# E table of an S5 layer on VectorE alone, and its output tables made during the latents' S5 projections

## The chip, the cores and the metric

The kernel runs on one core of one Trainium2 chip. The metric is the device time of one execution in microseconds (us); smaller is better. A core has a matrix engine (TensorE, "PE" in the rows, "PEld" for its weight loads), three elementwise engines (VectorE "DVE", ScalarE "ACT", GpSimd "POOL") and a queue engine (SyncE "SP") that issues the transfers (DMAs). Each engine works through its own instructions strictly in order and waits on the others through semaphores.

## The reference, cut to what matters

One layer of a diffusion backbone over 1024 latent tokens and 256 context tokens of width 1024: a half-step SwiGLU FFN, a mixer (a gated short convolution beside a bidirectional S5 state-space scan with 32 groups of 64 complex states), and a second FFN.

```python
x = half_step_ffn(x, mods[0:3], ...); ctx = half_step_ffn(ctx, mods_c[0:3], ...)
lam_bar = jnp.exp(lam * dt)
b_bar = ((lam_bar - 1.0) / lam)[:, :, None] * b
c_mat = lax.complex(c_re, c_im)
...
bu = jnp.einsum('blgh,gph->blgp', ug, b_bar)
_, h = lax.associative_scan(_linear_recurrence, (a, bu), axis=1, reverse=reverse)
y = einsum('blgp,ghp->blgh', states, c_mat).real + ... + d_skip * ug
...
x = half_step_ffn(x, mods[6:9], ...)
```

## The kernel before, in words

**Tiling.** Tokens are taken in chunks of 8, so the scan runs over 128 latent chunks (and 32 context chunks) instead of 1024 tokens. What a chunk does to the state and to the output is put into tables made from the S5 parameters: B (8 powers of lam_bar times b_bar), C (8 powers times c), E (32 x 4 powers that turn the scan into one over real magnitudes), F and T. B, C, E and F lie in one DRAM tensor, `pd`, in column ranges BO, CO, EO and FO, one block for each of 16 pairs of groups; T lies in `td`.

**Order of the work.** (1) `g_lat`, the latents' gate/up product of the first FFN. Each of 22 column blocks is seven products of 12 matmuls, since every fp32 operand is split into a high and a low half: ScalarE copies the high half (`w<-t`, `w<-wr` on ACT), VectorE subtracts it for the low half (the same names on DVE). Raw weights come by DMA into four buffers `wr`. (2) `g_ctx`, the same for the 256 context rows, with 24 matmuls of 256 columns for each 128 columns of weights. (3) The down products. (4) In `run`, `u_lat`: the latents' S5 inputs, two groups of four 24-matmul products, stored to `ud` and read back into `tb`; beside them `ctx_in` sums, norms, scales and transposes the context rows, and `u_ctx` projects them. (5) Convolution products with the 16 S5 pairs (`s5_pair`) between them; each pair loads its block of `pd`. (6) Output projection and second FFN.

**Where the tables are made.** `s5_params` is a generator that makes E and F and stores the powers (`pwd`) and b_bar (`brd`). `fill` in `run` advances it from inside `g_lat`: each `self.step(fills[m - 1])` asks for as many steps as FN holds for the product, 12 for a column block, and between two yields of `s5_params` stand SP[n] empty steps, before 1 and 2 in turn. For E eight iterations each make two halves of 128x512, `er` and `ei` (real and imaginary), with a temporary `xt`: six products or sums, on VectorE in even iterations and on GpSimd in odd ones, then two stores to `pd`. `er`, `ei` and `xt` are the same memory in every iteration. In the rows all of this is `tb<-tb 128x512` and `pd<-tb`. `s5_prep` makes B, T and then C, advanced from inside `g_ctx`. C is four iterations of six instructions of 128x1024 (`z<-z,z`), on VectorE and GpSimd in turn, with two stores each (`pd<-z`). T goes over DRAM: small stores `gd<-z`, then `td<-gd`.

**What sets the order.** The kernel is written as above, but a scheduler with a simulated timeline orders each engine's instructions from the dependences and priorities; `step` gives fill work lower priority. All DMAs here go through SP's one queue in order, so a DMA that waits holds up those behind it. All instructions are recorded through one helper, so every row says L51: rows are told apart by tiles (w split halves, wr raw weights, ps PSUM, t and z scratch, tb the five-row buffer).

Of the kernel before, what the change touches and what calls it, by code (L numbers as in the profile page):

```python
# [16 lines left out]
P = 128  # L17
D = 1024
# [8 lines left out]
H = 16  # L27
T8 = 8
# [40 lines left out]
class Kernel:  # L69
# [111 lines left out]
    def setup(self):  # L181
        nc, i = self.nc, self.i
        self.cp = self.pool("cp")
        self.dr = self.pool("dr", space=bass.MemoryType.DRAM)
        self.psum = self.pool("psum", bufs=8, space=bass.MemoryType.PSUM)
        self.sm = self.pool("sm", bufs=8)
        self.wp = self.pool("wp", bufs=6)
        self.tp = self.pool("tp", bufs=1)
        self.tb = self.t(self.tp, [P, 5 * D], "tb")
        self.ring([self.tb[:, D * k : D * k + D] for k in range(5)])  # L190
        self.wrs = [self.t(self.wp, [P, D], f"wr{k}", bufs=1) for k in range(4)]
        self.zp = self.pool("zp", bufs=32)

        dr = self.dr
        self.x1d = self.t(dr, [T8, CL, D], "x1d")
        self.x2d = self.t(dr, [T8, CL, D], "x2d")
        self.rowd = [self.t(dr, [KT, P], f"rowd{k}") for k in range(4)]
        self.pd = self.t(dr, [PAIRS, P, TO], "pd")
        self.pwd = self.t(dr, [P, D], "pwd")
        self.brd = self.t(dr, [P, D], "brd")  # L200
        self.gd = self.t(dr, [H, G, 15, H], "gd")
        self.td = self.t(dr, [P, G, P], "td")
        self.ud = self.t(dr, [G * H, T8, CL], "ud")
        self.ucd = self.t(dr, [G * H, T8, CC], "ucd")
        self.yd = self.t(dr, [T8, H, G, CL], "yd")
        self.zd = [self.t(dr, [P, NT], f"zd{k}") for k in range(4)]
        self.t1d = [self.t(dr, [P, 512], f"t1d{k}") for k in range(NF // 2)]
        self.t2d = [self.t(dr, [P, 512], f"t2d{k}") for k in range(NF // 2)]
        self.scd = [self.t(dr, [P, 4 * NC], f"scd{k}") for k in range(6)]
        self.sd = [[self.t(dr, [P, NT], f"sd{n}_{k}") for k in range(NF)] for n in range(2)]  # L210

        cp = self.cp
        rows = self.t2([16, P])
        self.load(rows[0:8, :], i["c"][0].rearrange("(k p) -> k p", p=P))
        self.load(rows[8:16, :], i["c_ctx"].rearrange("(k p) -> k p", p=P))
        self.ident = self.t(cp, [P, P], "ident")
        make_identity(self.tc.nc, self.ident)
        srow = self.t2([16, P])
        nc.scalar.activation(srow, rows, AF.Silu)
        pt = self.ps()  # L220
        self.tr(pt[:, :16], srow, 16)
        self.scol = self.t(cp, [P, 16], "scol")
        nc.vector.tensor_copy(self.scol, pt[:, :16])
        self.srep = self.t(cp, [P, KT, 32], "srep")
        nc.scalar.activation(
            self.srep.rearrange("p k (n c) -> p n c k", c=2),
            pt[:, :16].rearrange("p (c k) -> p c k", c=2).unsqueeze(1).to_broadcast([P, 16, 2, KT]), AF.Copy,
        )
        self.ones = self.t(cp, [P, 1], "ones")
        nc.gpsimd.memset(self.ones, 1.0)  # L230
        self.modc = {}
        self.mask = self.t(cp, [P, 2 * CL + 4], "mask", dt=mybir.dt.bfloat16)
        nc.gpsimd.memset(self.mask, 1.0)
        nc.gpsimd.memset(self.mask[:, :: CL + 1], 0.0)
# [939 lines left out]
    def s5_params(self):  # L1174
        nc, i = self.nc, self.i
        pl = nc.gpsimd
# [4 lines left out]
        def A(n):  # L1181
            v = arena[:, used[0] : used[0] + n]
            used[0] += n
            assert used[0] <= D
            return v
# [28 lines left out]
        e, em1, s, cm1 = A(64), A(64), A(64), A(64)  # L1214
# [8 lines left out]
        pw = pv[:, :576].rearrange("p (r m a) -> p r m a", r=2, m=9)  # L1223
# [88 lines left out]
        pdv = self.pd.rearrange("a p w -> p a w")  # L1312
        for r in range(2):
            for b in range(2):
                gs = slice(16 * b, 16 * b + 16)
# [19 lines left out]
        for b in range(8):  # L1335
            gs = slice(4 * b, 4 * b + 4)
            er, ei, xt = (
                u.rearrange("p (a m n) -> p a m n", a=4, m=4) for u in (ee[:, :512], ee[:, 512:], arena[:, :512])
            )
            shp = [P, 4, 4, 32]  # L1340
            x0 = e32[0][:, gs, :].unsqueeze(2).to_broadcast(shp)
            x1 = e32[1][:, gs, :].unsqueeze(2).to_broadcast(shp)
            v0 = vv[:, 0, :, gs].rearrange("p m a -> p a m").unsqueeze(3).to_broadcast(shp)
            v1 = vv[:, 1, :, gs].rearrange("p m a -> p a m").unsqueeze(3).to_broadcast(shp)
            self.cmul(er, ei, x0, x1, v0, v1, xt, pl if b % 2 else None)
            for r, m in ((0, er), (1, ei)):
                c0 = EO + 256 * r
                self.load(
                    pdv[:, 2 * b : 2 * b + 2, c0 : c0 + 256], m.rearrange("p (a q) m n -> p a (q m n)", q=2)
                )  # L1350
            yield
# [11 lines left out]
        shp = [P, T8, 32]  # L1363
# [18 lines left out]
    def s5_prep(self):  # L1382
        nc, i = self.nc, self.i
        pl = nc.gpsimd
        slot = lambda shape: self.t(self.zp, shape, "z")
# [4 lines left out]
        pw, br_ = slot([P, 2, 2, T8, 32]), slot([P, 2, 32, H])  # L1390
# [4 lines left out]
        ct = slot([P, 2, 32, H])  # L1395
# [4 lines left out]
        for k in range(2):  # L1400
# [4 lines left out]
            for d in range(2):  # L1405
                r = slice(64 * d, 64 * d + 64)
# [3 lines left out]
        pdv = self.pd.rearrange("a p w -> p a w")  # L1410
        shp = [P, 8, T8, H]

        def power(w, r, gs):
            return pw[:, w, r, :, gs].rearrange("p t a -> p a t").unsqueeze(3).to_broadcast(shp)

        for o in range(4):
            gs = slice(8 * o, 8 * o + 8)
            xr, xi, xt = slot(shp), slot(shp), slot(shp)
# [38 lines left out]
        for t in range(T8):  # L1457
            r = slice(t * H, t * H + H)
# [6 lines left out]
        for t in range(T8):  # L1465
            r = slice(t * H, t * H + H)
            self.load(self.td[r], self.gd[:, :, 7 - t : 15 - t].rearrange("h g l k -> h g (l k)"))
            if t % TY == TY - 1:
                yield
        for o in range(4):  # L1470
            gs = slice(8 * o, 8 * o + 8)
            mr, mi, xt = slot(shp), slot(shp), slot(shp)
            prb, pib = power(1, 0, gs), power(1, 1, gs)
            cr_ = ct[:, 0, gs, :].unsqueeze(2).to_broadcast(shp)
            ci_ = ct[:, 1, gs, :].unsqueeze(2).to_broadcast(shp)
            e = pl if o % 2 else None
            self.mul(mr, cr_, prb, e)
            self.mul(xt, ci_, pib, e)
            self.add(mr, mr, xt, e)
            yield  # L1480
            self.mul(mi, ci_, prb, e)
            self.mul(xt, cr_, pib, e)
            self.sub(mi, mi, xt, e)
            for r, m in ((0, mr), (1, mi)):
                c0 = CO + 256 * r
                self.load(
                    pdv[:, 4 * o : 4 * o + 4, c0 : c0 + 256], m.rearrange("p (a q) t h -> p a (q t h)", q=2)
                )
            yield
# [225 lines left out]
    def run(self):  # L1715
# [13 lines left out]
        xt = [self.z() for _ in range(4)]  # L1729
# [39 lines left out]
        h = self.hops(stages, bl, hb, hr)  # L1769
# [4 lines left out]
        def norm2():  # L1774
            ss = self.t(self.sm, [P, 4], "ss")
            for k in range(4):
                self.square(ss, k, xt2[k])
                yield
            r = yield from self.rsq_g(ss)
            yield  # L1780
            for k in range(4):
                self.scale(xt2[k : k + 1], r[:, k : k + 1], nc.scalar if k in X2A else None)
                yield

        def accs2():
            pt = self.ps()
            for kt in range(KT):
                for mod in range(2):
                    self.first_mm(pt, mod, kt, self.ws[kt][:, mod, :])
            yield  # L1790
            self.first_cols(1, pt)
            yield

        q, a = norm2(), accs2()
# [20 lines left out]
        def fill():  # L1815
# [10 lines left out]
            for n, _ in enumerate(self.s5_params()):  # L1826
                for _ in range(1 + SP[n % len(SP)]):
                    yield
# [86 lines left out]
        u = self.tb.rearrange("p (g c) -> p g c", g=G)  # L1915
        cx = ctx_in()
        next(cx)
        for _ in itertools.chain(self.u_lat(mhi, mlo, 0, u), self.u_lat(mhi, mlo, 1, u)):
            next(cx, None)
        for _ in cx:  # L1920
            pass
        self.u_ctx(chi2, clo2)
# [6 lines left out]
        z = [None] * 4  # L1929
# [103 lines left out]
        p = evac(0, self.out_group(ss[0], wo2))  # L2033
# [4 lines left out]
        p = evac(1, self.out_group(ss[1], wo2))  # L2038
# [7 lines left out]
        p = evac(2, acc)  # L2046
# [5 lines left out]
        h = self.hops(stages, bl, hb, hr)  # L2052
        next(h)
        next(p)
        p = evac(3, acc)
# [64 lines left out]
FW = 22  # L2120
FN = (2, 2, 1, 1, 2, 2, 2)
GAP = 6
SP = (1, 2)
UN2 = 3
EARLY2 = 4
TAIL = 3
# [47 lines left out]
```

## Time and profile before

| | |
|---|---|
| median of three runs | 2077.2 us (2076.4 to 2079.46) |
| the profiled execution | 2077.89 us |
| its span, first to last instruction | 2076.1 us |
| TensorE busy | 1961.8 us, 94% |
| VectorE busy | 1433.3 us, 69% |
| ScalarE busy | 825.3 us, 40% |
| GpSimd busy | 191.3 us, 9% |
| mean granted TensorE clock | 0.98 of 2.4 GHz |

The rows further down come from this one execution. "[2.25 <-ACT t L51]" at a row's end means: the engine stood idle for 2.25 us before this row and was released by ScalarE's instruction that wrote a tile t. A row with "xN" is N neighbouring instructions of one form merged; its time runs from the first start to the last end, and neighbours on one engine overlap a little.

### The profile page before, as it was taken

How to read it: one execution, taken by the hardware profiler on the slowest of the kernel's cores; microseconds unless marked ns; L12 is line 12 of the kernel's file. 1: busy time of each engine (PE TensorE's matmuls, PEld its weight loads, DVE VectorE, ACT ScalarE, POOL GpSimd, SP SyncE). 2: the span in 40 equal slices, each digit the busy share in tenths (PEclk: the TensorE clock that was granted, in tenths of full speed). 3: DMA queues.
4: the chain of work that ended last, by engine and by line, in shares of the span. 5: the costliest groups of instructions: out<-in, count | busy, mean ns of one | idle time of the engine just before them, and what ended most of it. 6: DMA issues, size and time to landing. Idle time of an engine off the chain costs nothing. (4 is left out here: it accounts for less than half of the span.)

```text
span 2076.1 us, 25812 instructions
## 1 busy us (share of the span) xinstructions
PE 1961.8 (94%) x9364; PEld 1562.7 (75%) x9364; DVE 1433.3 (69%) x2532; ACT 825.3 (40%) x1459; POOL 191.3 (9%) x106
## 2 busy tenths in 40 slices
PE   7899999989898999999998899997999999999997
PEld 3477778867898877777887778763788888887775
DVE  1874469787766679787528985486865555577977
ACT  5433333423343345566532334353333333334543
POOL 0000000040347000000003430010000000000000
PEclk9999999999999999999999999999999999999999
DMA  9167632445579977476665533134632322267554
GB/s 325 31 218 249 240 137 72 132 127 167 172 222 268 294 249 251 147 259 224 180 207 170 182 112 122 53 130 122 203 122 81 100 73 82 87 254 267 198 182 162
DMA packets 334059, 356.78 MB, mean 172 GB/s; under 512 B 47024, under 2 KB 248428, under 8 KB 333932
## 3 DMA queue, kind: packets, MB, share of 16 engines
q1 hardware_dynamic: 331628, 346.75, 51.4%
q10 hardware_dynamic: 2304, 8.39, 1.0%
q8 instruction: 73, 1.20, 0.2%
q14 instruction: 54, 0.44, 0.1%
HBM read 282.97 MB, written 74.17 MB: 172 GB/s over the span
## 5 line engine op out<-in xcount | busy, mean ns | idle before, releaser
L51 PE MATMUL ps<-z,w 128*128 128x512 f32 (+1 forms) x5328 | 1151.2, 377 | 39.6 <-DVE w L51 13.1
L51 PEld LDWEIGHTS ps<-z,w 128*128 128x128 f32 x5328 | 937.7, 192 | 236.4 <-DVE w L51 14.9
L51 PE MATMUL ps<-w,w 128*128 128x512 f32 x1848 | 427.3, 392 | 16.3 <-DVE w L51 9.7
L51 PEld LDWEIGHTS ps<-w,w 128*128 128x128 f32 x1848 | 346.4, 188 | 95.6 <-DVE w L51 14.7
L51 ACT ACTIVATE w<-wr 128x512 fp32r<-128x512 f32 (+1 forms) x270 | 206.6, 767 | 348.4 <-PE ps L51 281.7
L51 DVE TENSOR_TENSOR w<-wr,w 128x512 fp32r<-128x512 f32 (+1 forms) x264 | 246.9, 937 | 117.4 <-ACT w L51 110.8
L51 ACT ACTIVATE w<-t 128x512 fp32r<-128x512 f32 x292 | 177.1, 626 | 213.4 <-DVE t L51 129.9
L51 DVE TENSOR_TENSOR w<-t,w 128x512 fp32r<-128x512 f32 x292 | 198.6, 691 | 77.0 <-ACT w L51 76.6
L51 DVE TENSOR_TENSOR t<-t,ps 128x512 f32<-128x512 f32 x150 | 102.4, 684 | 97.6 <-PE ps L51 94.5
L51 PE MATMUL ps<-z,t 128*128 128x512 f32 x512 | 148.0, 449 | 11.4 <-DVE t L51 10.3
L51 ACT ACTIVATE t<-ps 128x512 f32<-128x512 f32 (+2 forms) x143 | 77.4, 542 | 166.3 <-PE ps L51 162.8
L51 PEld LDWEIGHTS ps<-z,t 128*128 128x128 f32 x512 | 96.8, 190 | 60.8 <-issue 36.2
L51 ACT ACTIVATE w<-z 128x512 fp32r<-128x512 f32 x110 | 69.6, 632 | 146.2 <-PE ps L51 144.0
L51 DVE TENSOR_TENSOR z<-z,z 128x512 fp32r<-128x512 f32 (+3 forms) x127 | 106.6, 869 | 15.5 <-ACT z L51 11.6
L51 DVE TENSOR_TENSOR t<-wr 128x512 f32<-128x512 f32 x140 | 94.2, 686 | 32.2 <-DMA wr<-in_ffn_w_gu 18.1
L51 ACT ACTIVATE t<-z 128x1024 bf16<-128x1024 f32 (+3 forms) x132 | 75.5, 605 | 47.2 <-DVE z L51 30.8
L51 DVE TENSOR_TENSOR w<-z,w 128x512 fp32r<-128x512 f32 x110 | 75.5, 686 | 26.6 <-ACT w L51 26.4
L51 POOL TENSOR_TENSOR z<-z,z 128x1024 f32<-128x1024 f32 x24 | 79.2, 3320 | 76.3 <-PE ps L51 42.0
L51 ACT ACTIVATE t<-t 128x512 f32<-128x512 f32 (+1 forms) x83 | 51.7, 623 | 78.6 <-DVE t L51 78.2
L51 DVE TENSOR_TENSOR z<-t,ps 128x512 f32<-128x512 f32 (+1 forms) x52 | 29.8, 573 | 64.9 <-PE ps L51 64.3
L51 POOL TENSOR_TENSOR tb<-tb 128x512 f32<-128x512 f32 x24 | 33.6, 1412 | 435.4 <-DMA sd<-z 409.0
L51 ACT ACTIVATE z<-z 128x512 fp32r<-128x512 f32 (+2 forms) x76 | 48.3, 673 | 56.7 <-DVE z L51 56.7
(121 smaller groups left out, 1402.1 us busy)
## 6 DMA issues: line engine op xcount, KB each, us to landing
wr<-in_ffn_w_gu SPq DMA_DIRECT2D x146, 512.0 KB, 4.1
wr<-in_ffn_w_down SPq DMA_DIRECT2D x198, 256.0 KB, 4.2
tb<-in_w_ada SPq DMA_DIRECT2D x56, 512.0 KB, 4.5
sd<-z SPq DMA_DIRECT2D x44, 512.0 KB, 3.0
z<-sd SPq DMA_DIRECT2D x88, 256.0 KB, 5.4
wr<-in_ffn_w_down SPq DMA_DIRECT2D x22, 512.0 KB, 4.9
wr<-in_w_in SPq DMA_DIRECT2D x20, 512.0 KB, 4.0
z<-in_w_ada SPq DMA_DIRECT2D x16, 512.0 KB, 6.3
```

The lines of the kernel that those rows point to most:

```text
L51: r = f(*a, **kw)
```

## The change

Three edits. (a) In the E loop of `s5_params` all six instructions are on VectorE, and a yield stands between the real and the imaginary half, so the loop has 16 yields instead of 8. SP becomes (1,): one empty step between all yields. (b) The C loop leaves `s5_prep` for a generator of its own, `s5_ctab`, with all its instructions on VectorE; c goes to a new DRAM tensor `ctd` and comes back with the powers. (c) `run` advances `s5_ctab` beside `u_lat` and `ctx_in`.

```diff
--- before.py
+++ after.py
@@ -198,6 +198,7 @@
         self.pd = self.t(dr, [PAIRS, P, TO], "pd")
         self.pwd = self.t(dr, [P, D], "pwd")
         self.brd = self.t(dr, [P, D], "brd")
+        self.ctd = self.t(dr, [P, D], "ctd")
         self.gd = self.t(dr, [H, G, 15, H], "gd")
         self.td = self.t(dr, [P, G, P], "td")
         self.ud = self.t(dr, [G * H, T8, CL], "ud")
@@ -1342,7 +1343,13 @@
             x1 = e32[1][:, gs, :].unsqueeze(2).to_broadcast(shp)
             v0 = vv[:, 0, :, gs].rearrange("p m a -> p a m").unsqueeze(3).to_broadcast(shp)
             v1 = vv[:, 1, :, gs].rearrange("p m a -> p a m").unsqueeze(3).to_broadcast(shp)
-            self.cmul(er, ei, x0, x1, v0, v1, xt, pl if b % 2 else None)
+            self.mul(er, x0, v0)
+            self.mul(xt, x1, v1)
+            self.sub(er, er, xt)
+            yield
+            self.mul(ei, x0, v1)
+            self.mul(xt, x1, v0)
+            self.add(ei, ei, xt)
             for r, m in ((0, er), (1, ei)):
                 c0 = EO + 256 * r
                 self.load(
@@ -1467,20 +1474,30 @@
             self.load(self.td[r], self.gd[:, :, 7 - t : 15 - t].rearrange("h g l k -> h g (l k)"))
             if t % TY == TY - 1:
                 yield
+        self.load(self.ctd, ct.rearrange("p r a h -> p (r a h)"))
+
+    def s5_ctab(self):
+
+        slot = lambda shape: self.t(self.zp, shape, "z")
+        pw, ct = slot([P, 2, T8, 32]), slot([P, 2, 32, H])
+        self.load(pw.rearrange("p r t a -> p (r t a)"), self.pwd[:, 512:])
+        self.load(ct.rearrange("p r a h -> p (r a h)"), self.ctd)
+        pdv = self.pd.rearrange("a p w -> p a w")
+        shp = [P, 8, T8, H]
+        yield
         for o in range(4):
             gs = slice(8 * o, 8 * o + 8)
             mr, mi, xt = slot(shp), slot(shp), slot(shp)
-            prb, pib = power(1, 0, gs), power(1, 1, gs)
+            prb, pib = (pw[:, r, :, gs].rearrange("p t a -> p a t").unsqueeze(3).to_broadcast(shp) for r in range(2))
             cr_ = ct[:, 0, gs, :].unsqueeze(2).to_broadcast(shp)
             ci_ = ct[:, 1, gs, :].unsqueeze(2).to_broadcast(shp)
-            e = pl if o % 2 else None
-            self.mul(mr, cr_, prb, e)
-            self.mul(xt, ci_, pib, e)
-            self.add(mr, mr, xt, e)
-            yield
-            self.mul(mi, ci_, prb, e)
-            self.mul(xt, cr_, pib, e)
-            self.sub(mi, mi, xt, e)
+            self.mul(mr, cr_, prb)
+            self.mul(xt, ci_, pib)
+            self.add(mr, mr, xt)
+            yield
+            self.mul(mi, ci_, prb)
+            self.mul(xt, cr_, pib)
+            self.sub(mi, mi, xt)
             for r, m in ((0, mr), (1, mi)):
                 c0 = CO + 256 * r
                 self.load(
@@ -1915,8 +1932,12 @@
         u = self.tb.rearrange("p (g c) -> p g c", g=G)
         cx = ctx_in()
         next(cx)
+        ctab = self.s5_ctab()
         for _ in itertools.chain(self.u_lat(mhi, mlo, 0, u), self.u_lat(mhi, mlo, 1, u)):
             next(cx, None)
+            next(ctab, None)
+        for _ in ctab:
+            pass
         for _ in cx:
             pass
         self.u_ctx(chi2, clo2)
@@ -2120,7 +2141,7 @@
 FW = 22
 FN = (2, 2, 1, 1, 2, 2, 2)
 GAP = 6
-SP = (1, 2)
+SP = (1,)
 UN2 = 3
 EARLY2 = 4
 TAIL = 3
```

The scheduler orders the engines anew. Three places, from the built programs (a number after an underscore names the buffer):

VectorE, start of the E table, before (`tb_72<-tb_72` are its instructions; the others belong to `g_lat`):

```order
L51 TENSOR_TENSOR tb_72<-tb_72 128x512 x3
L51 TENSOR_TENSOR z_3115<-t_508_3023,t_505_2977 128x512
L51 TENSOR_TENSOR tb_72<-tb_72 128x512
L51 TENSOR_TENSOR t_531_3184<-wr_4_75 128x512
L51 TENSOR_TENSOR tb_72<-tb_72 128x512 x2
L51 TENSOR_TENSOR w_3186<-t_531_3184,w_3186 128x512
L51 TENSOR_TENSOR t_519_3098<-t_519_3098,ps_3197 128x512
L51 TENSOR_TENSOR w_3213<-t_509_3025,w_3213 128x512
L51 TENSOR_TENSOR t_531_3184<-t_531_3184,wr_3_74 128x512
L51 TENSOR_TENSOR t_527_3142<-t_527_3142,ps_3085 128x512
L51 TENSOR_TENSOR w_3240<-t_531_3184,w_3240 128x512
L51 TENSOR_TENSOR w_3258<-wr_3_74,w_3258 128x512
```

and now:

```order
L51 TENSOR_TENSOR tb_72<-tb_72 128x512 x3
L51 TENSOR_TENSOR z_2992<-t_493_2893,t_490_2847 128x512
L51 TENSOR_TENSOR tb_72<-tb_72 128x512
L51 TENSOR_TENSOR t_516_3057<-wr_5_76 128x512
L51 TENSOR_TENSOR tb_72<-tb_72 128x512
L51 TENSOR_TENSOR t_504_2968<-t_504_2968,ps_3067 128x512
L51 TENSOR_TENSOR tb_72<-tb_72 128x512
L51 TENSOR_TENSOR w_3059<-t_516_3057,w_3059 128x512
L51 TENSOR_TENSOR w_3083<-t_494_2895,w_3083 128x512
L51 TENSOR_TENSOR tb_72<-tb_72 128x512 x2
L51 TENSOR_TENSOR t_516_3057<-t_516_3057,wr_2_73 128x512
L51 TENSOR_TENSOR t_512_3016<-t_512_3016,ps_2955 128x512
```

Before, six instructions come within nine rows of the first and then none until the next even iteration; now the table goes on through the whole stretch, about one instruction of the table to one of `g_lat`.

SyncE in `g_ctx`, around T's transfers, before:

```order
L51 DMA z_5138<-sd_9_61_135 128x512
L51 DMA z_5140<-z_4327 16x32x16
L51 DMA gd_89<-z_4327 512x1x16 x7
L51 DMA gd_89<-z_5140 512x1x16
L51 DMA z_5158<-sd_10_62_136 128x512
L51 DMA wr_4_75<-in_ffn_w_gu 128x8x128
L51 DMA td_90<-gd_89 512x128 x8
L51 DMA wr_5_76<-in_ffn_w_gu 128x8x128
L51 DMA wr_2_73<-in_ffn_w_gu 128x8x128
L51 DMA wr_3_74<-in_ffn_w_gu 128x8x128
L51 DMA pd_86<-z_5232 128x4x256
L51 DMA wr_4_75<-in_ffn_w_gu 128x8x128
```

and now:

```order
L51 DMA z_5139<-sd_9_62_136 128x512
L51 DMA z_5141<-z_4328 16x32x16
L51 DMA gd_90<-z_4328 512x1x16 x6
L51 DMA wr_4_75<-in_ffn_w_gu 128x8x128
L51 DMA gd_90<-z_5141 512x1x16
L51 DMA z_5159<-sd_10_63_137 128x512
L51 DMA wr_5_76<-in_ffn_w_gu 128x8x128
L51 DMA wr_2_73<-in_ffn_w_gu 128x8x128
L51 DMA td_91<-gd_90 512x128 x8
L51 DMA wr_3_74<-in_ffn_w_gu 128x8x128
L51 DMA wr_4_75<-in_ffn_w_gu 128x8x128
L51 DMA wr_5_76<-in_ffn_w_gu 128x8x128
```

The first weight load (`wr_4_75`) moves ahead of the last `gd` store and of one `z<-sd` load, the next two (`wr_5_76`, `wr_2_73`) ahead of the eight `td` loads, and the `pd` stores of C are gone.

VectorE in the S5 projections, from the residual sum of the context rows on, before (`sy` and `sq` are steps of the norm, `z_7802` and `z_7803` the rows that are scaled and then transposed):

```order
L51 SCALAR_TENSOR_TENSOR sy_8597<-sq_8596,sy_8594 128x2
L51 TENSOR_TENSOR sq_8596<-sy_8597 128x2
L51 SCALAR_TENSOR_TENSOR sq_8596<-sq_8596,sv_8593 128x2
L51 SCALAR_TENSOR_TENSOR sy_8598<-sq_8596,sy_8597 128x2
L51 TENSOR_SCALAR z_7802<-z_7802,sy_8598 128x1024
L51 TENSOR_SCALAR z_7803<-z_7803,sy_8598 128x1024
L51 TENSOR_TENSOR w_8635<-wr_4_75,w_8634 128x1024
L51 TENSOR_TENSOR w_8818<-wr_5_76,w_8817 128x1024
L51 TENSOR_TENSOR z_8435<-t_1374_8690,z_8433 128x256
L51 TENSOR_TENSOR w_8851<-wr_2_73,w_8850 128x1024
L51 TENSOR_TENSOR z_8435<-t_1377_8723,z_8433 128x256
```

and now, the last part ahead of the scaling and what follows it (`z_7760`, `z_7761` are the rows; `z<-z_8469,z_8468` are products of C):

```order
L51 SCALAR_TENSOR_TENSOR sq_8569<-sq_8568 128x2
L51 TENSOR_TENSOR z_8648<-z_8648,z_8650 128x1024
L51 SCALAR_TENSOR_TENSOR sy_8570<-sq_8569,sy_8567 128x2
L51 TENSOR_TENSOR z_8650<-z_8469,z_8468 128x1024
L51 TENSOR_TENSOR sq_8569<-sy_8570 128x2
L51 SCALAR_TENSOR_TENSOR sq_8569<-sq_8569,sv_8566 128x2
L51 SCALAR_TENSOR_TENSOR sy_8571<-sq_8569,sy_8570 128x2
L51 TENSOR_SCALAR z_7760<-z_7760,sy_8571 128x1024
L51 TENSOR_SCALAR z_7761<-z_7761,sy_8571 128x1024
L51 TENSOR_TENSOR w_8857<-wr_2_73,w_8856 128x1024
L51 TENSOR_TENSOR z_8393<-t_1374_8680,z_8391 128x256
L51 TENSOR_TENSOR z_8649<-z_8469,z_8468 128x1024
```

Sixteen instructions of C stand between the residual sum and the scaling, the weight split `w_8857` comes before the first `z<-t` low half, and further instructions of C stand between the low halves.

## Rows read from the trace of the kernel before

**Rows 1.** Page, part 1: busy us, share of the span and instructions of each engine.
```profile
PE 1961.8 (94%) x9364; PEld 1562.7 (75%) x9364; DVE 1433.3 (69%) x2532; ACT 825.3 (40%) x1459; POOL 191.3 (9%) x106
```

**Rows 2.** Timeline of PE, 394-510 us: start, length, engine, instruction, count, idle before it.
```profile
394.71 35.03 PE L51 MATMUL ps<-z,w 128*128 128x512 f32 x150
432.00 5.85 PE L51 MATMUL ps<-z,w 128*128 128x512 f32 x24 [2.25 <-ACT t L51]
442.81 50.22 PE L51 MATMUL ps<-z,w 128*128 128x512 f32 x204 [4.97 <-DVE t L51]
495.21 7.36 PE L51 MATMUL ps<-z,w 128*128 128x512 f32 x24 [2.18 <-DVE t L51]
```

**Rows 3.** Stretches: length, busy us of PE, PEld, DVE, ACT, POOL, granted clock, DMA share, GB/s.
```profile
440.00:450.00 10.00, 7.19 (x20) 5.72 (x21) 9.22 (x14) 1.82 (x4) 3.07 (x3) 0.66 0.36 88
...
650.00:660.00 10.00, 5.91 (x30) 5.42 (x29) 10.00 (x10) 1.33 (x2) 10.00 (x1) 0.66 1.05 299
```

**Rows 4.** Groups by form, POOL, 400-480 us: forms, count, busy us, mean ns, idle before.
```profile
L51 POOL TENSOR_TENSOR tb<-tb 128x512 f32<-128x512 f32 x24 | 33.6, 1412 | 435.4 <-DMA sd<-z 409.0 <-DVE tb L51 16.2 <-DMA pd<-tb 9.4
```

**Rows 5.** Stretches: the whole stretch of the E table, 405-470 us.
```profile
405.00:470.00 65.00, 57.78 (x237) 46.10 (x236) 55.17 (x67) 19.99 (x35) 32.99 (x24) 0.95 0.45 130
```

**Rows 6.** Groups by form, DVE, 405-470 us.
```profile
L51 DVE TENSOR_TENSOR w<-wr,w 128x512 fp32r<-128x512 f32 x10 | 12.4, 1237 | 3.1 <-ACT w L51 3.1
...
L51 DVE TENSOR_TENSOR t<-t,ps 128x512 f32<-128x512 f32 x9 | 6.1, 677 | 0.8 <-PE ps L51 0.8
```

**Rows 7.** Groups by form, DVE, 340-400 us.
```profile
L51 DVE TENSOR_TENSOR w<-wr,w 128x512 fp32r<-128x512 f32 x9 | 6.2, 688 | 3.3 <-ACT w L51 3.2
```

**Rows 8.** Timeline of DVE: three neighbours at 405 us, six at 648 us.
```profile
405.35 1.90 DVE L51 TENSOR_TENSOR tb<-tb 128x512 f32<-128x512 f32 x3
...
647.64 6.88 DVE L51 TENSOR_TENSOR z<-z,z 128x1024 f32<-128x1024 f32 x6
```

**Rows 9.** Tile pd, 405-475 us: GpSimd's waits (us, times) for its stores, and their landing.
```profile
  POOL tb L51: 9.4, 3
...
DMA to landing us min/median/max: 2.1/3.2/3.7
```

**Rows 10.** Waits of PE, 650-700 us: us in total, times, longest.
```profile
PE ps L51 <- ACT w L51: 6.8, 4, 3.6
PE ps L51 <- DVE w L51: 5.5, 4, 3.2
```

**Rows 11.** Timeline of PE, 637-672 us.
```profile
637.06 13.77 PE L51 MATMUL ps<-z,w 128*128 128x256 f32 x114
...
655.71 7.41 PE L51 MATMUL ps<-z,w 128*128 128x256 f32 x44 [0.45 <-DVE w L51]
...
667.32 4.42 PE L51 MATMUL ps<-z,w 128*128 128x256 f32 x24 [1.67 <-ACT w L51]
```

**Rows 12.** Groups by form, DVE, 644-680 us.
```profile
L51 DVE TENSOR_TENSOR w<-wr,w 128x1024 fp32r<-128x1024 f32 x7 | 13.9, 1985 | 2.5 <-ACT w L51 2.5
```

**Rows 13.** Timeline of SP's queue, 641-661 us.
```profile
641.97 6.17 SPq L51 DMA_DIRECT2D gd<-z  x8
...
648.84 0.43 SPq L51 DMA_DIRECT2D wr<-in_ffn_w_gu  x1
...
656.02 4.77 SPq L51 DMA_DIRECT2D wr<-in_ffn_w_gu  x3
```

**Rows 14.** Timeline of DVE, 1014-1047 us.
```profile
1014.41 2.71 DVE L51 SCALAR_TENSOR_TENSOR z<-z,sy,z 128x1024 f32<-128x1024 f32 x2
...
1020.12 1.41 DVE L51 TENSOR_SCALAR z<-z,sy 128x1024 f32<-128x1024 f32 x2
...
1045.66 1.22 DVE L51 TENSOR_TENSOR w<-wr,w 128x1024 fp32r<-128x1024 f32 x1 [4.69 <-ACT w L51]
```

**Rows 15.** Timeline of PE, 1038-1062 us.
```profile
1038.81 0.38 PE L51 MATMUL ps<-ident,z 128*128 128x128 f32 x2
...
1055.00 7.02 PE L51 MATMUL ps<-z,w 128*128 128x256 f32 x56 [0.99 <-ACT z L51]
```

## The prediction, made before the changed kernel ran

> **What bounds the kernel now.** I read the page's first part, then the waits of TensorE by stretch, then the timelines of the engine that ended each wait. TensorE is busy for 94% of the span, VectorE for 69%, GpSimd for 9% [rows 1]. So time can only be won where TensorE stands still or runs at a lower clock, and lost where something new makes it stand. The change works in three places: (A) the gate/up product of the first FFN, where the E table is made (405 to 470 us); (B) the context's gate/up product, where the C table is made (640 to 680 us); (C) the latents' S5 projections, where the C table goes (1005 to 1062 us).
>
> In A TensorE runs 150 matmuls in 35.03 us (0.2335 each), then waits 2.25 and 4.97 us, and the 204 matmuls behind these waits take 50.22 us (0.2462 each); both waits end with something that VectorE or ScalarE hands over [rows 2]. The mean granted clock in the ten microseconds of the longer wait is 0.66 of full speed [rows 3]. The lower pace costs 204 x 0.0127 = 2.6 us, and 0.2 us on the 24 matmuls between the waits. At stake in A: 2.25 + 4.97 + 2.8 = 10.0 us.
>
> In B the waits of TensorE sum to 6.8 us for ScalarE's weight halves and 5.5 us for VectorE's [rows 10]. Undisturbed, 114 matmuls take 13.77 us (0.1208 each); after the first wait 44 take 7.41 us instead of 5.3, and later 24 take 4.42 instead of 2.9 [rows 11], with a granted clock of 0.66 again, so partly at 1.2 and partly at 2.4 GHz [rows 3]. At stake in B: 12.3 + 2.1 + 1.5 = 15.9 us.
>
> In C TensorE is nearly without a gap: one wait of 0.99 us [rows 15].
>
> **Part A, the E table.** Removed: 24 GpSimd products of 128x512, 33.6 us busy, mean 1412 ns [rows 4]. They cost VectorE too. While they run, VectorE's weight split with both operands in SBUF takes 1237 ns, the sum that reads PSUM 677 ns [rows 6]; the same split takes 688 ns when GpSimd rests [rows 7]. In sum, 67 instructions of 128x512 kept VectorE busy for 55.17 us [rows 5]; at the pitch of three in 1.90 us, (1.90 - 0.69)/2 = 0.605 us [rows 8], they need 40.5. So GpSimd cost VectorE 14.7 us.
>
> The Trainium skill's page "SBUF — State Buffer", section "Who interferes with whom", says that a VectorE instruction with two SBUF inputs contends with a GpSimd instruction that reads SBUF, and that whichever comes second blocks until the first is through. The trace agrees on who is hit and who is not. By the rule alone each of the 24 would block VectorE for its whole length, 33.6 us; the trace shows 14.7, since VectorE also has PSUM work and idle time beside them.
>
> Added: the same 24 products on VectorE, 24 x 0.605 = 14.5 us. So VectorE's work over the table stays as it was within 0.2 us. What changes is its density. A column block takes 84 matmuls (7 products of 12), 84 x 0.2335 = 19.6 us, calls the filler 12 times, and needs 16 VectorE instructions of its own (7 splits, 4 sums of weights, 5 evacuations), 9.7 us. Before, 8 yields cost 2 or 3 calls in turn, 20 calls = 1.67 blocks = 32.7 us of TensorE, in which VectorE owed 14.5 + 16.2 + 14.7 = 45.4 us: 12.7 too much, and TensorE lost 10.0, so a cushion of 2.7 was used up. After, 16 yields cost 2 calls each, 32 calls = 2.67 blocks = 52.3 us, with 29.0 + 25.9 = 54.9 us on VectorE: 2.6 too much, which the cushion takes.
>
> The added wait: a half of the table is overwritten while its store to the table in DRAM may still run, and now VectorE itself waits, with the weight splits and evacuations that TensorE needs queued behind. Between the end of a half and the next write to it stand about seven rows, 7 x 0.605 = 4.2 us; a store lands 3.2 us after issue in the median, 3.7 at most, yet GpSimd waited 9.4 us for three of them [rows 9], because the queue was held up ahead of the store. I put 2 us in all on TensorE for such waits. A gives 10.0 - 2 = 8 us. Bounds: 14 us (all of it, and the 2.18 us wait with 1.8 us of lower clock at 495 us [rows 2], which a VectorE without arrears would spare) and -2 us. The denser steps ahead of the table are covered: VectorE has gaps there (3.3 us before the splits alone [rows 7]); without cover they cost up to 2 us, inside that bound.
>
> **Part B, the C table leaves.** Removed: 12 GpSimd and 12 VectorE products of 128x1024, 12 x 1.134 = 13.6 us of VectorE [rows 8], and eight 512 KB stores; added one 512 KB store. Without them VectorE's weight split, 1985 ns there [rows 12], has no neighbour, and the six products that stood 6.88 us ahead of a split [rows 8] are gone. What stays late is the first wait: ScalarE's half came from a weight load issued at 648.84 us, behind eight gd stores that took 6.17 us to issue [rows 13]. It now stands ahead of the last gd store and a z<-sd load (0.77 and 0.70 us), so 1.5 us earlier: 3.6 becomes 2.1. The next two weight loads, issued at 656.02 us behind td, now stand ahead of td. I leave 2.1 us of wait, 1.5 of lower clock behind it, and 0.3: B gives 15.9 - 3.9 = 12 us. Bounds: 4 us (if DMA made all of ScalarE's waits: then only 5.5 less what is left goes) and 16 us.
>
> **Part C, the C table arrives.** Added: 24 VectorE products, 24 x 1.134 = 27.2 us, two loads (the tables back from DRAM) and eight stores in SP's queue. Sixteen products stand ahead of the scaling of the context rows. The residual sum ends at 1014.41 + 2.71 = 1017.1 us [rows 14]. Then 16 x 1.134 = 18.1, two weight splits (2.3), nine small instructions (about 1.9) and the first scaling (0.75) end at 1040.2 us. TensorE transposes those rows at 1038.81 us [rows 15]: 1.4 us late. Behind the scaling VectorE waits in order for the split that ran at 1045.66 us [rows 14], then four products stand between the low halves of context blocks 0 and 1, and three more with a split ahead of block 2. Followed row by row, the third projection's low weight half comes 1.9 us late and block 2's low half 1.0 us, while the old 0.99 us wait is contained in these. C costs 1.4 + 1.9 + 1.0 - 1.0 = 3.3, taken as 3 us. Bounds: 0 (if the order leaves slack that I don't see) and 10 (if the table loads land after 1017 us, each microsecond is passed on, and the 5 us of idle behind the scaling are lost as well). The stores have cover: all eight stand in SP's queue ahead of the context's projections' own stores, which the S5 stage waits for in any case; the weight loads behind them are for the convolution, which starts after the context's projections. Without that cover each microsecond of SP would be one of TensorE's, within the same bound.
>
> **Sum.** -8 - 12 + 3 = -17 us. The profiled execution took 2077.9 us (span 2076.1), 0.7 above the median of the three runs, 2077.2. So 2060.9 by its own time, 2060.2 against the median; I say 2060.
>
> **Rivals.** (1) DMA, not GpSimd, makes B's waits. For: ScalarE's halves are 6.8 of the 12.3 us, and they hang on loads. Against: their queue place improves and 3.5 MB of stores leave. B gives 4, sum -9: 2068.
> (2) C costs its upper bound, the tables arriving late: -8 - 12 + 10 = -10: 2067. For: 1 MB of context rows is loaded just ahead of the tables. Against: both loads are issued before the residual sum ends, and nothing in SP's queue holds them up but those rows.
> (3) GpSimd blocks VectorE for its whole length. Then 33.6 us of arrears go in A for 14.5 us of new work, TensorE gets all that is at stake, A gives its 14 and B its 16, and the sum is -27: 2050. For: the splits at 1237 and 1985 ns [rows 6, 12]. Against: 14.7 us were measured [rows 5]. (This is the rule of the page "SBUF — State Buffer" of the Trainium skill, taken by itself.)
> (4) The other side: E's own stores. VectorE waits at 14 reuses of a half, while before GpSimd took half of these waits. If issue and landing take 6.2 us instead of 3.6, each costs 2 us: 28 us more in A, less the 2 assumed: sum -17 + 26 = +9: 2086. It decides from 17/14 = 1.2 us each, a store landing 5.4 us after its half is done. For: 9.4 us of GpSimd's waits; against: no store there landed later than 3.7 us.
> (5) Gains and losses cancel, say A nothing, B 7, C 6: 2076.
>
> **Chances.** Forecast 0.50 (2055 to 2065), (1) 0.14, (2) 0.13, (3) 0.11, (4) 0.05, (5) 0.07. A change of 0.2% is 4.2 us, about what a measurement can tell from none: faster is below 2073, slower above 2081.4. Faster: 0.50 + 0.12 + 0.11 + 0.11 = 0.84; within 0.2%: 0.10; slower: 0.06. The range 2051 to 2073 leaves out most of (3), (4) and (5).
>
> **What would show it.** In the changed profile GpSimd has 36 instructions fewer; VectorE's splits in A and B stand near 690 and 1220 ns; TensorE has no wait of 5 us near 440; one wait of about 2 us near 650 (earlier by what A gave), and none of 3 us after it; new waits of 1 to 2 us at the context transposes and in the context's S5 projections. Waits of VectorE for pd stores of more than 10 us in sum, or a wait above 5 us in C, would make the prediction wrong.

## The result, and the profile after

The changed kernel takes 2046.9 us (median of 4 runs, 2046.4 to 2049.5), the kernel before 2078.1 us (four runs; three gave the 2077.2 of the forecast): a ratio of 0.985, 95% interval 0.984 to 0.987. The forecast was 2060 us: right in direction, but the gain came out 13 us larger, and the measured time lies below the low end of the range (2051). The profiled execution of the changed kernel took 2049.5 us, the slowest of the four, so the traces hold 28.4 us of the 31.2 us between the medians.

The page of the changed kernel, first part (answers to [rows 1]):

```profile
PE 1950.0 (95%) x9364; PEld 1554.6 (76%) x9364; DVE 1430.8 (70%) x2568; ACT 825.8 (40%) x1459; POOL 111.7 (5%) x70
```

The same work on VectorE in sum, 80 us less on GpSimd (36 instructions gone, as the prediction named it), 12 us less on TensorE: lower clock that is no more. By stretches of the program, each from one fixed TensorE instruction to the next (us; the second begins at 548.1 us before, at 529.5 now, 14 us behind the first matmuls of 256 columns; "rest" is what follows the S5 projections, and the 290 us ahead of `g_lat` are in no column but the span):

| | `g_lat` from 290 us | `g_ctx` | down products | S5 projections | rest | span |
|---|---|---|---|---|---|---|
| before | 258.4 | 163.1 | 294.0 | 87.7 | 983.3 | 2076.1 |
| after | 239.6 | 151.9 | 292.5 | 92.2 | 981.6 | 2047.7 |
| gained | 18.8 | 11.1 | 1.5 | -4.6 | 1.7 | 28.4 |

Before and after are one execution each, the profiled one.

**A.** Timeline of TensorE (start, length, instruction, count, idle before it), then stretches (length, busy us of PE, PEld, DVE, ACT, POOL, granted clock, DMA share, GB/s), then VectorE by form (390 to 455 us); they answer to [rows 2], [rows 3, 5] and [rows 6]:

```profile
389.71 98.70 PE L51 MATMUL ps<-z,w 128*128 128x512 f32 x424
```
```profile
440.00:450.00 10.00, 10.00 (x45) 8.11 (x44) 8.90 (x16) 4.04 (x7) 0.00 (x0) 1.00 0.72 232
...
405.00:470.00 65.00, 65.00 (x281) 52.69 (x281) 60.33 (x102) 24.43 (x41) 0.00 (x0) 1.00 0.60 175
```
```profile
L51 DVE TENSOR_TENSOR w<-wr,w 128x512 fp32r<-128x512 f32 x12 | 8.2, 686 | 0.4 <-ACT w L51 0.4
```

TensorE runs 424 matmuls without a gap, at 0.2328 us each and at full clock. VectorE does 102 instructions in the 65 us where it did 67, and its splits are back at 686 ns. Two waits of the kernel before that go with the three in [rows 2] are gone too:

```profile
504.81 0.33 PE L51 MATMUL ps<-ident,z 128*128 128x128 f32 x1 [2.24 <-DVE z L51]
505.47 0.55 PE L51 MATMUL ps<-ident,z 128*128 128x128 f32 x3 [0.34 <-DVE z L51]
```

**B.** Waits of TensorE, 535 to 690 us (total, times, longest), and its timeline (answer to [rows 10, 11]):

```profile
PE ps L51 <- DVE w L51: 6.1, 2, 5.7
PE ps L51 <- ACT w L51: 4.1, 1, 4.1
```
```profile
542.39 4.64 PE L51 MATMUL ps<-z,w 128*128 128x256 f32 x22 [5.68 <-DVE w L51]
...
646.75 0.79 PE L51 MATMUL ps<-z,w 128*128 128x256 f32 x2 [4.05 <-ACT w L51]
648.01 33.54 PE L51 MATMUL ps<-z,w 128*128 128x256 f32 x262 [0.47 <-DVE w L51]
```

Of the eight waits behind 650 us only the first two are left, and the first is not smaller. The 5.68 us at 542 us stood in the kernel before too (5.82 at 561 us). The weight load that the 4.05 us wait hangs on was issued behind the `td` loads, as SyncE's queue shows:

```profile
631.69 7.12 SPq L51 DMA_DIRECT2D td<-gd  x8
638.91 9.44 SPq L51 DMA_DIRECT2D wr<-in_ffn_w_gu  x5
```

Ten microseconds of the kernel before ran at a lower clock with no wait ahead of them since 561 us, and have no counterpart now:

```profile
590.00:600.00 10.00, 10.00 (x76) 10.00 (x76) 8.31 (x7) 2.34 (x4) 3.89 (x2) 0.83 0.76 228
```

**C.** Timeline of TensorE in the S5 projections (answers to [rows 15]), and a stretch of it:

```profile
1009.00 0.30 PE L51 MATMUL ps<-ident,z 128*128 128x128 f32 x1 [1.43 <-DVE z L51]
...
1025.27 1.38 PE L51 MATMUL ps<-z,w 128*128 128x256 f32 x7 [1.47 <-ACT z L51]
1027.27 8.07 PE L51 MATMUL ps<-z,w 128*128 128x256 f32 x53 [0.62 <-DVE z L51]
```
```profile
1020.00:1030.00 10.00, 7.89 (x51) 7.09 (x50) 10.00 (x14) 6.11 (x14) 0.00 (x0) 0.88 0.81 256
```

The transposes are 1.43 us late and block 2's low half makes a wait of 0.62 us, both as foreseen in kind. The wait of 1.9 us for the third projection's low weight half is not there; in its place the old wait for ScalarE's half has grown from 0.99 to 1.47 us.

### The profile page after: what moved, and what is told of

It is laid out like the page before. It is cut to its first block, busy times and chain, and to the rows that moved or that the text cites. A ratio compares the mean times of both kernels' runs of the same rounds, so it can differ in the third digit from the quotient of the medians.

```text
span 2047.7 us, 25792 instructions
## 1 busy us (share of the span) xinstructions
PE 1950.0 (95%) x9364; PEld 1554.6 (76%) x9364; DVE 1430.8 (70%) x2568; ACT 825.8 (40%) x1459; POOL 111.7 (5%) x70
## 4 chain that ended last, share of the span: by engine, by line
PE 72%; DVE 16%; DMA 5%; issue 3%; ACT 2%; SPq 1%; POOL 1%; DVEq 0%; ACTq 0%; POOLq 0%
PE ps L51 72%; DVE z L51 7%; DVE t L51 6%; DVE w L51 3%; DMA wr<-in_ffn_w_gu 1%; SPq L51 1%; DMA wr<-in_ffn_w_down 1%; DMA z<-in_w_ada 1%; ACT t L51 1%; ACT w L51 1%; DMA wr<-t2d 0%; ACT z L51 0%; DMA z<-in_x 0%; POOL t L51 0%; DMA z<-scd 0%
## 5 line engine op out<-in xcount | busy, mean ns | idle before, releaser
L51 PE MATMUL ps<-w,w 128*128 128x512 f32 x1848 | 427.0, 391 | 14.9 <-DVE w L51 8.8
L51 DVE TENSOR_TENSOR w<-wr,w 128x512 fp32r<-128x512 f32 (+1 forms) x264 | 233.9, 887 | 122.6 <-ACT w L51 120.2
L51 DVE TENSOR_TENSOR z<-z,z 128x512 fp32r<-128x512 f32 (+3 forms) x139 | 114.6, 857 | 17.0 <-ACT z L51 11.6
L51 PE MATMUL ps<-w,t 128*128 128x512 f32 x264 | 64.4, 401 | 1.9 <-DVE w L51 1.3
L51 ACT ACTIVATE z<-ps 128x512 f32<-128x512 f32 x74 | 41.6, 595 | 56.7 <-PE ps L51 51.4
```

Source lines behind the costliest of these rows:

```text
L51: r = f(*a, **kw)
```

## The experiments

All times are medians against the kernel before, with the 95% interval of the ratio. The stretches are those of one execution each, the profiled one, which lies up to 3.7 us from its median (us):

| | `g_lat` | `g_ctx` | down | S5 proj. | rest | ratio |
|---|---|---|---|---|---|---|
| e1 E part alone | 239.6 | 160.8 | 292.5 | 87.5 | 987.2 | 0.991 (0.988 to 0.993) |
| e2 C part alone | 259.4 | 157.2 | 292.5 | 90.6 | 982.6 | 0.998 (0.997 to 0.999) |
| e3 E engine alone | 243.8 | 165.7 | 290.9 | 87.6 | 982.1 | 0.992 (0.991 to 0.994) |
| e4 E spread alone | 252.2 | 157.9 | 292.8 | 87.5 | 984.4 | 0.996 (0.994 to 0.997) |
| e6 idle GpSimd | 254.3 | 153.2 | 295.2 | 90.3 | 980.5 | 0.993 (0.991 to 0.994) |
| e7 B on VectorE | 239.6 | 149.7 | 293.1 | 92.2 | 983.4 | 0.986 (0.985 to 0.988) |
| e8 C behind the norm | 239.6 | 153.6 | 292.4 | 98.2 | 985.6 | 0.992 (0.991 to 0.993) |
| e9 gd on ScalarE's queue | 239.6 | 151.6 | 293.0 | 91.8 | 981.9 | 0.985 (0.983 to 0.987) |
| e10 both of these | 239.6 | 148.4 | 294.2 | 90.1 | 979.9 | 0.984 (0.982 to 0.985) |
| e11 and C's loads first | 239.6 | 148.0 | 291.8 | 95.3 | 978.6 | 0.986 (0.984 to 0.988) |
| e12 C in place, VectorE | 239.6 | 160.5 | 293.1 | 87.5 | 982.4 | 0.988 (0.986 to 0.990) |
| e13 T on GpSimd's queue | 239.6 | 139.3 | 294.7 | 90.5 | 981.9 | 0.980 (0.979 to 0.982) |

**The parts.** e1 is the E hunk and `SP = (1,)` alone, e2 the rest of the diff alone.

> The E table's part of the change alone (all six instructions on VectorE, 16 yields, one empty step between them); C stays in the context's gate/up product as before. In the changed kernel the stretch from the first undisturbed latent product (290.0 us) to the first matmul of the context's product (548.1 before, 529.5 now) became 18.8 us shorter: 12.0 us of waits and 6.8 us of lower clock. Theory S (spreading): the gain is that stretch's own, so this kernel takes about 2078 - 18.8 = 2059 us. Rival: part of it came with C's departure (fewer transfers, another order); then it stays above 2064 us.

> The C table's part alone: C in its own generator beside the latents' S5 projections, on VectorE alone; E is made as before. In the changed kernel the context's gate/up product became 11.1 us shorter and the S5 projections 4.6 us longer, and other stretches 3 us shorter. If the two parts add up, this kernel takes 2078 - 11.1 + 4.6 = 2071.5 us, down to 2068 us if the other stretches' 3 us belong to it; if B's gain needed the earlier end of A, it stays within 4 us of 2078 us.

Measured: 2058.9 us (2052.7 to 2063.7, a wide spread) and 2073.6 us. A is that stretch's own: 239.6 us in every kernel that has the new E table, whatever else it does (e6 apart, which adds work to the stretch). e2 came out between its two outcomes: B by itself gave 5.9 us in its trace, C cost 2.9; that is 5 us less in `g_ctx` than in the changed kernel. The trace of e2 shows where: the wait that is 4.05 us in the changed kernel is 5.34 us, and twice the clock is lower while TensorE is busy throughout (590 to 600 us at 0.84, 630 to 640 us at 0.72):

```profile
630.00:640.00 10.00, 10.00 (x68) 10.00 (x67) 2.07 (x3) 2.88 (x5) 0.00 (x0) 0.72 0.83 231
```

**What in A does it.** e3 changes one argument; e4 is the E hunk and `SP = (1,)` with GpSimd kept in odd iterations. e3:

```diff
-            self.cmul(er, ei, x0, x1, v0, v1, xt, pl if b % 2 else None)
+            self.cmul(er, ei, x0, x1, v0, v1, xt, None)
```

> E's odd iterations on VectorE instead of GpSimd and nothing else: six instructions in one step, 8 yields, one and two empty steps in turn, C as before. Theory S: the table still asks 29.0 + 16.2 = 45 us of VectorE in 33 us of TensorE, as much as before (14.5 + 16.2 + 14.7 of contention), so the waits near 430 to 500 us stay: 2078 us, within 4 us. Rival G (GpSimd itself is the cause, by contention and by holding SP's queue for 18.2 us): the waits go, 2059 to 2063 us.

> The spreading alone: a yield between real and imaginary halves, one empty step between all yields, but odd iterations stay on GpSimd; C as before. Theory S: VectorE owes 14.5 + 25.9 + about 14.7 of contention = 55 us in 52 us of TensorE, what the changed kernel owes too, and the table begins 17 us earlier: 2059 to 2064 us. Rival G: GpSimd's products still make the splits 1.2 us long and hold SP's queue, so the waits stay: above 2072 us.

Measured: 2061.4 and 2068.9 us. Theory S, that density is the cause (the ledger of the prediction), falls: with the bursts as they were, taking GpSimd out gives 14.6 us of A's 18.8. Density still counts for something: spreading with GpSimd gives 6.2 (e4 lies between the two outcomes foreseen for it), and 4.2 without it (e1 against e3). Stretches 390 to 490 us of before and of e3, and e3's waits of TensorE from 390 to 530 us:

```profile
390.00:490.00 100.00, 92.78 (x387) 74.45 (x387) 82.40 (x114) 38.17 (x62) 33.65 (x24) 0.97 0.57 162
```
```profile
390.00:490.00 100.00, 99.97 (x431) 80.82 (x430) 92.76 (x162) 43.48 (x71) 0.00 (x0) 1.00 0.59 175
```
```profile
PE ps L51 <- DVE z L51: 2.0, 2, 1.6
```

VectorE was busy for 82 of 100 us before and TensorE starved; in e3 it is busy for 93 and TensorE waits for nothing up to 490 us. So VectorE lacked no time over the stretch: it had it at the wrong moments. Two rows of VectorE before, and one group (by form, 395 to 550 us):

```profile
426.82 1.29 DVE L51 TENSOR_TENSOR tb<-tb 128x512 f32<-128x512 f32 x2 [2.69 <-DMA pd<-tb]
428.03 1.57 DVE L51 TENSOR_TENSOR w<-wr,w 128x512 fp32r<-128x512 f32 x1
```
```profile
L51 DVE TENSOR_TENSOR tb<-tb 128x512 f32<-128x512 f32 x30 | 21.5, 736 | 4.0 <-DMA pd<-tb 2.7 <-POOL tb L51 1.0 <-DMA tb<-in_ssm_b_re 0.3
```

The split takes 1.57 us beside GpSimd, while the table's own 30 instructions on VectorE are hardly longer than undisturbed (736 ns against 686): they take turns with GpSimd's on the same memory, for which GpSimd waited 16.2 us [rows 4]. And VectorE stood still for 2.69 us until a store of a half had landed, with the split two table instructions behind. Another rival is SyncE's queue, which stood 18.2 us for GpSimd's halves. Its waits, 400 to 480 us, first before and then in e3:

```profile
SPq L51 <- POOL tb L51: 18.2, 8, 5.8
SPq L51 <- DVE tb L51: 12.1, 7, 3.3
```
```profile
SPq L51 <- DVE tb L51: 31.6, 18, 5.0
```

In e3 the queue stands for halves as long as before (31.6 us against 30.3) and TensorE doesn't wait there, so the queue's standing by itself does not make the waits. To take contention by itself (theory K: VectorE and GpSimd hold each other up where both read SBUF), e6 puts idle work back on GpSimd in the changed kernel, 48 products of half the size that nothing depends on:

```diff
+        dum = arena[:, 512:768].rearrange("p (a m n) -> p a m n", a=2, m=4)
...
+            if b % 2:
+                for x, v_ in ((x0, v0), (x1, v1), (x0, v1)) * 4:
+                    self.mul(dum, x[:, :2], v_[:, :2], pl)
```

> The changed kernel with idle work put back on GpSimd: in E's odd iterations 12 products of 128x256 each, 48 in all (as many elements as the 24 of 128x512 that left it), into a spare corner that nobody reads and no transfer touches. Theory K (contention at SBUF is the main cost): VectorE's two-SBUF instructions beside them go from 690 towards 1200 ns; VectorE is 93% busy in this stretch, so of 15 to 33 us of loss TensorE pays 10 to 20 us: 2057 to 2067 us. Theory Q (GpSimd cost by what waited for its results: SP's queue, the next half, the context rows behind the table): under 4 us, 2047 to 2051 us.

Measured: 2062.1 us, 15.2 us more than the changed kernel, 14.7 of them in `g_lat`. Its timelines of TensorE, GpSimd and VectorE (two rows), and the stretch, first of e6 and then of the changed kernel:

```profile
400.41 22.51 PE L51 MATMUL ps<-z,w 128*128 128x512 f32 x84 [3.50 <-DVE t L51]
428.05 75.60 PE L51 MATMUL ps<-z,w 128*128 128x512 f32 x312 [5.12 <-DVE t L51]
```
```profile
381.28 0.64 POOL L51 TENSOR_TENSOR tb<-tb 128x256 f32<-128x256 f32 x1 [379.67 <-ACT tb L51]
385.96 49.35 POOL L51 TENSOR_TENSOR tb<-tb 128x256 f32<-128x256 f32 x47 [4.04 <-issue]
```
```profile
391.22 1.12 DVE L51 TENSOR_TENSOR t<-wr 128x512 f32<-128x512 f32 x1
...
393.30 0.68 DVE L51 TENSOR_TENSOR t<-t,ps 128x512 f32<-128x512 f32 x1
```
```profile
390.00:440.00 50.00, 41.38 (x155) 32.52 (x154) 50.00 (x58) 12.74 (x22) 42.02 (x43) 0.86 0.33 100
```
```profile
390.00:440.00 50.00, 50.00 (x217) 40.55 (x216) 47.61 (x79) 18.73 (x32) 0.00 (x0) 1.00 0.45 137
```

Theory K holds: nothing waits for a result of GpSimd, no transfer is added, and 8.6 us of waits are back with 6.1 us of lower pace. The products ran as one burst from 386 us on, into a stretch in which the changed kernel's VectorE had only 2.4 us of idle time left in 50. VectorE did 58 instructions in 50.0 us; at [rows 8]' pitch of 0.605 they need 35.1. So 42.0 us of GpSimd cost VectorE 14.9 us.

Those 42.0 us hold what GpSimd lost itself: a product took 0.64 us by itself and 49.35/47 = 1.05 from one to the next beside VectorE. By its undisturbed length (43 x 0.64 = 27.5 us) VectorE lost 0.54 us per us of GpSimd. In the kernel before it is much the same, by GpSimd's products (ns, shortest, median and longest):

```profile
L51 POOL TENSOR_TENSOR tb<-tb x24: 1075/1468/1806, 410.6 to 468.9; 128x512 f32<-128x512 f32 x24
```

One with no operation of VectorE beside it took 1.08 us, 24 of that length are 25.9 us, and VectorE lost 14.7, or 0.57. The rule that the second one blocks until the first is through (the Trainium skill, "SBUF — State Buffer", section "Who interferes with whom") agrees on who is hit, an operation with a PSUM input staying at 0.68 us, but as a price of GpSimd's whole length it gives too much.

**What in B does it.** e12 is e1 with `e = None` in C's loop; e7 takes GpSimd out of the B octets:

> E as in the changed kernel, C left in the context's gate/up product but all on VectorE. Theory K (GpSimd's contention makes B's waits): VectorE's splits beside C run at 1.2 us; C's 24 products, 27 us, find room between them, the stage takes about 155 us instead of 160.8 with GpSimd, and the S5 stage stays at 87.6: 2047 to 2052 us, near the changed kernel without moving anything. Rival: it is the volume of C in that place (VectorE's bursts of six ahead of a split, the eight stores in SyncE's queue) that makes the waits: 2057 us or more.

> The changed kernel with the B octets of odd index (12 products of 128x1024) on VectorE as well, so that GpSimd is idle in the context's gate/up product. The wait of 5.7 us for VectorE's split at 542 us falls where GpSimd's first six products run. Theory K: it goes, with about 3 us of lower clock behind it: 2047 - 8 = 2039 us. Rival: the wait is made by VectorE's own six products of 1.13 us ahead of the split (6.8 us); then it stays and the next octet adds one of the same kind: 2047 to 2053 us.

Measured: 2052.5 and 2048.7 us. e12's time lies between its two outcomes, but the stretch speaks for the rival: `g_ctx` takes 160.5 us, as with GpSimd in e1 (160.8). Of the 6.4 us between the medians of e1 and e12 the traces hold most behind the S5 projections (987.2 against 982.4 us), which was not followed up. VectorE and TensorE of e12:

```profile
630.20 12.56 DVE L51 TENSOR_TENSOR z<-z,z 128x1024 f32<-128x1024 f32 x11
642.68 1.20 DVE L51 TENSOR_TENSOR w<-wr,w 128x1024 fp32r<-128x1024 f32 x1
```
```profile
643.94 10.19 PE L51 MATMUL ps<-z,w 128*128 128x256 f32 x70 [4.19 <-DVE w L51]
```

Eleven products ahead of one split. B's gain is that C left, not that GpSimd fell silent; whether C's products or its eight stores in SyncE's queue weigh more, no run takes apart. In e7 the 5.7 us wait went, as theory K says, but waits of 2.48 and 3.75 us for ScalarE's halves came at 631 and 641 us, and the time stayed, though not for the reason that the rival gave.

**The wait that is left in B.** e9 issues T's `gd` stores from ScalarE's queue, e10 does so together with e7, e13 issues all of T's transfers from GpSimd's, with e7:

```diff
-                self.load(self.gd[:, :, 14 - t], kt_[r, :, 0:H])
+                nc.gpsimd.dma_start(self.gd[:, :, 14 - t], kt_[r, :, 0:H])
```

> The changed kernel with T's gd stores issued by ScalarE's queue instead of SyncE's. If the wait of 4.05 us for ScalarE's weight half at 647 us comes from weight loads that stand behind these stores in SyncE's queue, it shrinks to under 2 us and the lower clock behind it with it: 2043 to 2045 us. Rival: issuing costs ScalarE what it saved SyncE, and the weight halves come late all the same: 2046 to 2050 us.

> The changed kernel with both: B's octets of odd index on VectorE, and T's gd stores issued by ScalarE's queue. With B alone the wait of 5.7 us went, but waits of 1.5, 2.5 and 3.75 us came at 600 to 641 us, two of them for ScalarE's weight halves whose loads stand behind the gd stores. If SyncE's queue makes them, they shrink to 2 us together: 2048.7 - 6 = 2042 us. Rival: the td loads, which stay in SyncE's queue, hold the weight loads just as long: 2046 to 2050 us.

> The changed kernel with B's octets of odd index on VectorE, and all of T's transfers (16 gd stores and 8 td loads) issued by GpSimd's queue, which has nothing else to do there; with gd on ScalarE's queue the wait for ScalarE's weight half behind T's transfers was still 5.2 us. If that wait comes from what stands ahead of the weight loads in SyncE's queue, it goes with the lower clock behind it: 2044.6 - 5 = 2039 to 2041 us. Rival: the wait is ScalarE's or the transfers' own (the DMA engines are at 0.9 and more of their time there), whoever issues them: 2043 to 2047 us; or GpSimd's issuing costs VectorE at SBUF: above 2047 us.

Measured: 2047.2, 2044.6 and 2038.6 us (2033.2 to 2039.0, five runs). In e9 the 4.05 us wait has become three of 1.6, 0.7 and 0.8, and yet no time is won (`g_ctx` 151.6 us against 151.9); in e10 5.2 us of wait stay; ScalarE's row of e10 says why:

```profile
627.85 0.38 ACT L51 ACTIVATE t<-ps 128x256 f32<-128x256 f32 x1 [8.96 <-DMA gd<-z]
```

ScalarE stood for 9 us behind its own stores, and the td loads stayed ahead of the weights. In e13 TensorE's waits, 530 to 690 us, are:

```profile
PE ps L51 <- DVE z L51: 1.5, 1, 1.5
PE ps L51 <- DVE w L51: 1.2, 2, 0.7
```

The first two and the last of GpSimd's `td` loads:

```profile
673.66 0.64 POOL L51 DMA_DIRECT2D td<-gd  x1 [5.37 <-DMA gd<-z]
680.96 0.62 POOL L51 DMA_DIRECT2D td<-gd  x1 [6.66 <-issue]
...
714.86 0.62 POOL L51 DMA_DIRECT2D td<-gd  x1 [3.53 <-issue]
```

All waits for weight halves of some length are gone and `g_ctx` falls to 139.3 us, 10.4 less than in e7, which differs by the queue of T's transfers alone. So T's transfers ahead of the weight loads made them. That it was their place in SyncE's queue, and not their load on the DMA engines, is not shown apart: GpSimd issued them so slowly that the `td` loads came at 674 to 715 us, behind the stretch. e13 beats both kernels: 0.980 against 0.985, the intervals apart.

**What C costs.** e8 advances C only when the context's norm is through, e11 is e10 with C's loads ahead of the context rows':

```diff
-            next(cx, None)
-            next(ctab, None)
+            if next(cx, cx) is cx:
+                next(ctab, None)
```

> The changed kernel with the C generator advanced only when the context's norm steps are through: its 24 products stand behind the scaling of the context rows, among the context's projections. If the 4.6 us by which the latents' S5 stage became longer come from the products ahead of the scaling and between the low halves (waits of 1.4, 1.5 and 0.6 us and the clock behind them), most of it returns: 2043 to 2045 us. Rival: the eight stores then come later in SP's queue, ahead of weight loads of the convolution and of the pairs' own loads, and the S5 stage pays: 2047 to 2053 us.

> As the run before, and the C generator started ahead of the context rows' loads, so that its two table loads are first in the queue and its first products stand in VectorE's gaps ahead of the residual sum. If what C costs is the late scaling (transposes 1.43 us late) and the products between the low halves (1.5 and 0.6 us), some 2 to 3 us return: 3 us under the run before. Rival: the residual sum itself now stands behind nine products, and the scaling comes later still: the S5 stage grows by 2 us or more.

Measured: 2061.3 and 2047.1 us; the rivals hold in both, in e8 with 8 us more than the rival's upper bound (2053). TensorE in e8, and in e11:

```profile
1075.39 2.47 PE L51 MATMUL ps<-tb,z 128*128 128x160 f32 x8 [7.22 <-DMA z<-pd]
```
```profile
1008.28 0.45 PE L51 MATMUL ps<-ident,z 128*128 128x128 f32 x1 [4.81 <-DVE z L51]
```

Later, the first S5 pair waits 7.22 us for its block of `pd`; earlier, the scaling itself is late by 4.81 us. The place in between costs least of the three.

## Why the prediction was wrong

- **A, the term that failed: forecast 8 us, measured 18.8, bound 14.** Of the 258.4 us, 12.0 were waits (2.25 + 4.97 + 2.18 + 2.24 + 0.34) and 6.8 lower pace; all of it went. The prediction put 10.0 at stake, kept 2.0 back for store waits, and let the waits at 495 to 505 us into the bound alone, and there only the first of three. The step that failed is the ledger: as much work for VectorE in a denser or sparser stretch, the 14.7 us of contention counted like any other work, and due within 33 us before and 52 after. e3 refutes that: 24 products in GpSimd's stead, in the same bursts, leave TensorE 2.0 us of waits in that stretch instead of 12.0. Work of the table can be put off (it took 65 us before, as [rows 5] already said, and 66 after); a split that is stretched from 0.69 to 1.24 us holds TensorE up. e6 shows it from the other side: 14.9 us lost by VectorE are 14.7 lost by TensorE, there in a stretch in which VectorE had 2.4 us to spare. How much of the 14.6 us of e3 is contention, and how much the handing over of halves between two engines (VectorE's 2.69 us for a store), no run took apart.
- **The 2 us of store waits** stayed on VectorE: 1.1 us in two waits, and the stores landed in 2.3 us in the median (3.2 in [rows 9]); TensorE waited for none. Rival 4 is out.
- **Rival 3 gave 2050 us, nearest of all, by luck**: it rested on 33.6 us of arrears in VectorE, a sum that holds GpSimd's own losses, and the runs show 14.7. Its A of 14 and B of 16 were off by 4.8 and 4.9 us in opposite directions.
- **B: forecast 12, measured 11.1**, right in size, in part by luck. Its working had faults that cancelled: the first wait was to shrink to 2.1 us and stands at 4.05, since the weight loads at 638.91 us still stood behind the td loads (7.12 us in the queue); and with the pace behind it (33.54 us for 262 matmuls that need 31.65) 6.4 us are left, not 3.9; but a lower clock from 590 to 600 us before (0.83), which it had not counted, is absent now. That C's leaving, not GpSimd, was the cause is shown by the stretch in e12. Rival 1 was half right: what is left hangs on T's transfers ahead of the weight loads (e13).
- **C: forecast -3, measured -4.6**. The new waits sum to 2.5 us (1.43 + 1.47 + 0.62 less the old 0.99) against 3.3 worked out; the other 2 us are pace behind them, a clock of 0.88 and 0.95 in the ten microseconds from 1020 and from 1030 us, for which nothing had been put down.
- **Not in the sum**: 3.2 us in the down products and behind the S5 projections. One wait of 1.44 us at 795 us became 0.40; the rest was not followed up.

## What to carry to other kernels

Work of two kinds shares an in-order engine: what the matrix engine waits for, and filler. Count what a neighbour engine adds to the first kind in full, and filler at nothing as long as the engine has idle time in the stretch (e3: 14.5 us of it cost TensorE no wait there); a sum over both hides the stall. Before moving a product to the idle engine, look at what else it could do: here GpSimd was worth more as an issuer of small DMAs that nobody was in a hurry for (e13) than as a second multiplier.

## What the runs showed of the hardware

- DMAs issued from ScalarE's queue held that engine: it stood 8.96 us behind 9 gd stores (e10). GpSimd took 2.5 to 7.3 us from one of T's transfers to the next (e13), and only GpSimd itself waited, 5.37 us ahead of the first td load.
- VectorE and GpSimd hold each other up, not one the other: in e6 VectorE's operations with both inputs in SBUF went from 0.69 to 1.12 us, GpSimd's from 0.64 to 1.05 from one to the next, and VectorE's with a PSUM input stayed at 0.68.
- The granted clock fell to 0.72 of full speed, a mean over 2.4 and 1.2 GHz, in ten microseconds in which TensorE was busy throughout (e2, 630 to 640 us), with no wait of TensorE since 563 us. What set it off stays open.
